# The two tiles of normed activations begin at 96 instead of 160 modulo 256 bytes

## The chip, the cores and the metric

The kernel runs on one core of a Trainium2 chip. The metric is the device time of one execution in microseconds (us). The engines are named as in the profile: PE is TensorE (matrix products), PEld its loading of weights, DVE VectorE, ACT ScalarE, POOL GpSimd, and SP the engine that issues most of the loads. On-chip memory has 128 partitions; a tile takes the same bytes of each, and an address below is a byte address inside a partition. "Residue" means that address modulo 256.

In a product, one operand is loaded into the array as weights (128 rows, up to 128 columns) and the other, the moving operand, streams past it (up to 512 columns).

## The reference

One decoder layer for 256 tokens of 1024 channels in float32: a half-weighted SwiGLU block, a mixer of two parallel branches, and a second SwiGLU block. Each has a norm in front and one behind.

```python
h = h + 0.5 * rmsnorm(swiglu(rmsnorm(h, ffn1_pre_g), w_gate, w_up, w_down), ffn1_post_g)
u = rmsnorm(h, mix_pre_g)
z, xbc, dt_raw, q, k, v, gate_logits = split(u @ w_in)       # 1024 x 10272
y_ssd = ssd_branch(z, xbc, dt_raw, ...)                       # state-space branch, 2048 wide
y_att = diff_attn_branch(q, k, v, ...)                        # differential attention, 8 heads
gates = sigmoid(gate_logits + gate_b)
h = h + rmsnorm((gates[0] * y_ssd + gates[1] * y_att) @ w_out, mix_post_g)
h = h + 0.5 * rmsnorm(swiglu(rmsnorm(h, ffn2_pre_g), ...), ffn2_post_g)
```

`swiglu(x) = (silu(x @ w_gate) * (x @ w_up)) @ w_down` with an inner width of 2816.

## The kernel before

Each product is computed in three parts for precision: both operands are split into a high part, rounded to the type fp32r, and the low rest, and high x high, high x low and low x high are added in PSUM. The weights come from DRAM in 122 chunks of 1 MB, each into one of 3 buffers of the group `raw` (8192 bytes per partition). ACT rounds a chunk to `whi` (line 167) and DVE subtracts to get `wlo` (line 168), two tiles each of 4096 bytes in the group `k4`, which has 29 buffers. Chunks are taken in one fixed order, with loads three chunks ahead and splits about three. PE's order is written out by hand in most stages.

The normed activations, transposed so that channels lie on partitions, stand in two tiles of the group `u8`, 8192 bytes each: `u0` has channels 0 to 511, `u1` the rest. Their shape is [128, 4, 2, 256]: four channel blocks, then the high and the low part, then 256 tokens. So the high and the low part of a block lie next to each other, and a matmul can stream 512 columns, both parts, or only the 256 of one. `new_u` allocates the pair anew for each of the three stages, `f1`, `mx` and `f2`. The second half of the attention's output also uses a buffer of this group, late in the mixer.

Four forms of product read u:

- `mm_w` (lines 215 to 218, tiles `pg_f` and `pup_f`): the FFN's gate and up products from the third chunk of 256 columns on. For each half m of the chunk's 256 columns, and for each of 8 channel blocks, the weights `whi` (128 columns) with 512 moving columns of u (line 216), and `wlo` with the 256 of the high part (line 215, or 218 for the first block).
- `mm_t` (lines 201, 202, 204, tiles `pbc`, `pxs`, `pz`, `pq`, `pk`): the mixer's products that are wanted transposed. Weights `whi` or `wlo`, 256 moving columns of u.
- `mm_nat` (line 231, tiles `pn_f`, `pn_mx`, `pgt`): u is loaded as weights, 128 tokens at a time, and 512 columns of `whi` or `wlo` stream. The same line also serves `pws` and `pwd`, which read the branches' outputs instead of u, and part of `pn_f`, which reads `raw_u`, a copy in `k4`.
- the time-step product `pdt` (lines 692 to 694): weights of 32 columns, `wdt_h` and `wdt_l`, 256 moving columns of u. Its weights of one channel block begin 128 bytes behind those of the block before.

The down product (`acc_f`, line 441) reads `gh_f` and `gl_f` of `k4` as weights and streams 512 columns of `whi` or `wlo`; it does not read u. Transposes on PE load the tile to be turned as weights and stream the identity matrix `ident`.

At the start, POOL builds `ident` and other constants, then computes the first norm's scale (lines 330 and 331) from sums that ACT and DVE make, and scales the second token block.

The built program places the tiles as follows (first byte of each buffer; residue modulo 256 in brackets):

```
                          before                 after
ident                     26240 (128)            the same
h                         18048 (128)            the same
raw, 3 buffers            35744 ... (160)        the same
gap0, 192 bytes           -                      60320 (160)
u8, 2 buffers             60320, 68512 (160)     60512, 68704 (96)
gap1, 64 bytes            -                      76896 (96)
k4, 29 buffers            76704 ... (160)        76960 ... (160)
squares, 2 buffers        195808 ... (224)       196064 ... (224)
k2, 7 buffers             200224 ... (32)        200480 ... (32)
k3, 3 buffers             214560 ... (32)        214816 ... (32)
```

So "all other tiles" of the change's title are the large ones that hold weights and activations, `raw` and `k4`; the constants and the small groups have residues of their own and keep them. All residues in the table are multiples of 32; those of u and the weights are 32 modulo 64 before and after.

Of the kernel before, what the change touches and what calls it, by code (L numbers as in the profile page):

```python
# [14 lines left out]
F32 = mybir.dt.float32  # L15
# [9 lines left out]
P = 128  # L25
# [23 lines left out]
def tile_hybrid_layer(ctx: ExitStack, tc: tile.TileContext, x, ffn1_pre_g, ffn1_w_gate, ffn1_w_up,  # L49
# [4 lines left out]
    nc = tc.nc  # L54
    const = ctx.enter_context(tc.tile_pool(name="const", bufs=1))
    sb = ctx.enter_context(tc.tile_pool(name="sb", bufs=1))
# [254 lines left out]

    uT = [None] * 2

    def new_u(tag):
        for i in range(2):
            uT[i] = sb.tile([P, 4, 2, T], F32R, tag="u8", name=f"u{i}_{tag}", bufs=2)

    act_u = (lambda j: uT[j // 4][:, j % 4, 0, :], lambda j: uT[j // 4][:, j % 4, 1, :],
             lambda j: uT[j // 4][:, j % 4, :, :])
# [146 lines left out]
    class Norm:  # L466
# [3 lines left out]
        def __init__(self, tag, g):  # L470
            self.tag, self.g, self.pus = tag, g, []
            new_u(tag)
            self.to0 = in_u(0)
            self.dr = None
            self.left = []
# [717 lines left out]
```

## Time and profile before

| | |
|---|---|
| median of 3 runs | 754.04 us (753.83 to 754.93) |
| profiled execution, first to last instruction | 753.1 us |
| PE busy | 743.7 us, 4377 matmuls |
| PEld busy | 646.1 us, 4377 loads |
| DVE, ACT, POOL busy | 521.7, 440.1, 38.2 us |
| granted clock of PE | 0.999 |
| bytes moved by DMA | 137.96 MB |

The median of the runs stands 0.94 us above the profiled execution's span, which has no time of its own beside that span; sums are made against the span and carried over with this difference.

How to read it: PE's matmuls are pipelined, so the recorded duration of one is longer than the distance from its start to the next one's start. What counts for the time is the distance. A group's row gives the number of instructions and the mean duration; a tile's rows give the minimum, median and maximum. A timeline row merges neighbours of the same kind; its first number is the start of the first.

### The profile page before, as it was taken

Reading aid. Unit: us, or ns where it says so; the run is one execution under the profiler, and the core shown is the slowest. Engines: PE = TensorE matmul, PEld = TensorE weight load, DVE = VectorE, ACT = ScalarE, POOL = GpSimd, SP = SyncE. Lnnn points to the kernel's source line nnn. Section 1 sums busy time; section 2 is a strip of 40 time slices with the busy share of each in tenths; the row PEclk is TensorE's granted clock in tenths of the full one; section 3 lists DMA queues with packets and bytes.
Section 4 is the critical chain, followed back from the end, with each engine's and each line's share of the span. In section 5 each row is a group of like instructions: output and inputs, shape, how many; then the busy total and the mean of one; then the engine's idle time right before and its main releaser. Section 6 shows DMA issues by size and latency. Waiting matters only on the chain.

```text
span 753.1 us, 11054 instructions
## 1 busy us (share of the span) xinstructions
PE 743.7 (99%) x4377; PEld 646.1 (86%) x4377; DVE 521.7 (69%) x792; ACT 440.1 (58%) x737; POOL 38.2 (5%) x72
## 2 busy tenths in 40 slices
PE   8999999999999999999999999999999999999996
PEld 6888888888889999898999788788888888888885
DVE  6686677654577978767778988695684867766612
ACT  7475566643565565858966556784463756565511
POOL 6400000000300000000000000000010000000000
PEclk9999999999999999999999999999999999999999
DMA  8685765587253556565555463467361776555701
GB/s 300 161 265 182 224 224 207 200 286 228 64 166 116 174 163 215 165 210 176 187 168 177 165 219 127 153 224 251 112 225 56 224 224 217 173 173 183 290 1 56
DMA packets 94212, 137.96 MB, mean 183 GB/s; under 512 B 2684, under 2 KB 68304, under 8 KB 94160
## 3 DMA queue, kind: packets, MB, share of 16 engines
q1 hardware_dynamic: 91488, 129.51, 52.5%
q0 software_dynamic: 2368, 7.22, 3.1%
q8 instruction: 34, 0.56, 0.3%
q10 hardware_dynamic: 304, 0.53, 0.2%
q14 instruction: 18, 0.15, 0.1%
HBM read 136.17 MB, written 1.08 MB: 182 GB/s over the span
## 4 chain that ended last, share of the span: by engine, by line
PE 96%; DVE 1%; DMA 1%; POOL 1%; ACT 1%; issue 0%; SPq 0%; DVEq 0%; POOLq 0%
PE acc_f L441 16%; PE pup_f L216 9%; PE pg_f L216 9%; PE pws L231 6%; PE pgt L231 6%; PE pn_f L231 5%; PE pg_f L215 4%; PE pup_f L215 4%; PE acc_mx L441 3%; PE pn_mx L231 3%; PE pwd L231 3%; PE pxs L204 2%; PE pxs L202 2%; PE pxs L201 2%; PE pz L204 2%; PE pz L201 2%
## 5 line engine op out<-in xcount | busy, mean ns | idle before, releaser
L168 DVE TENSOR_TENSOR wlo<-raw,whi 128x1024 fp32r<-128x1024 f32 (+1 forms) x246 | 291.6, 1214 | 56.3 <-ACT whi L167 53.6
L167 ACT CAST whi<-raw 128x1024 fp32r<-128x1024 f32 (+1 forms) x246 | 247.3, 1044 | 59.9 <-PE acc_f L441 21.8
L216 PE MATMUL pg_f<-u_f,whi 128*128 128x512 f32 x288 | 101.2, 396 | 0.0
L216 PE MATMUL pup_f<-u_f,whi 128*128 128x512 f32 x288 | 101.1, 396 | 0.0
L215 PE MATMUL pg_f<-u_f,wlo 128*128 128x256 f32 x252 | 70.5, 280 | 0.0
L215 PE MATMUL pup_f<-u_f,wlo 128*128 128x256 f32 x252 | 70.3, 279 | 0.0
L216 PEld LDWEIGHTS pg_f<-u_f,whi 128*128 128x128 f32 x288 | 52.9, 188 | 9.7
L216 PEld LDWEIGHTS pup_f<-u_f,whi 128*128 128x128 f32 x288 | 52.7, 188 | 9.8
L441 PE MATMUL acc_f<-whi,gh_f 128*128 128x512 f32 x176 | 58.2, 390 | 0.0
L441 PE MATMUL acc_f<-wlo,gh_f 128*128 128x512 f32 x176 | 58.1, 389 | 0.0
L441 PE MATMUL acc_f<-whi,gl_f 128*128 128x512 f32 x176 | 58.1, 389 | 0.0
L215 PEld LDWEIGHTS pg_f<-u_f,wlo 128*128 128x128 f32 x252 | 47.5, 188 | 1.7
L215 PEld LDWEIGHTS pup_f<-u_f,wlo 128*128 128x128 f32 x252 | 47.5, 189 | 1.6
L220 DVE TENSOR_TENSOR su_f<-pup_f,su_f 128x256 f32<-128x256 f32 x36 | 15.2, 423 | 38.7 <-ACT su_f L219 38.7
L441 PEld LDWEIGHTS acc_f<-whi,gl_f 128*128 128x128 f32 x176 | 33.0, 188 | 6.9
L441 PEld LDWEIGHTS acc_f<-wlo,gh_f 128*128 128x128 f32 x176 | 33.0, 188 | 6.8
L441 PEld LDWEIGHTS acc_f<-whi,gh_f 128*128 128x128 f32 x176 | 33.0, 188 | 6.8
L231 PE MATMUL pgt<-whi,u_mx 128*128 128x512 f32 x128 | 34.8, 400 | 0.0
L201 PE MATMUL pz<-u_mx,whi 128*128 128x256 f32 x128 | 32.3, 288 | 0.0
L202 PE MATMUL pz<-u_mx,whi 128*128 128x256 f32 x128 | 31.8, 284 | 0.0
L201 PE MATMUL pxs<-u_mx,whi 128*128 128x256 f32 x128 | 31.7, 285 | 0.0
L202 PE MATMUL pxs<-u_mx,whi 128*128 128x256 f32 x128 | 31.4, 283 | 0.0
(318 smaller groups left out, 1425.9 us busy)
## 6 DMA issues: line engine op xcount, KB each, us to landing
raw<-in_w_in_dram SPq DMA_DIRECT2D x40, 1024.0 KB, 5.4
raw<-in_ffn_w_down_dram SPq DMA_DIRECT2D x22, 1024.0 KB, 5.3
raw<-in_ffn_w_gate_dram SPq DMA_DIRECT2D x20, 1024.0 KB, 5.7
raw<-in_ffn_w_up_dram SPq DMA_DIRECT2D x20, 1024.0 KB, 6.1
raw<-in_ssd_w_branch_dram SPq DMA_DIRECT2D x8, 1024.0 KB, 5.0
acb<-acd POOLq DMA_DIRECT2D x8, 512.0 KB, 4.9
raw<-in_da_w_branch_dram SPq DMA_DIRECT2D x4, 1024.0 KB, 5.1
raw<-in_w_out_dram SPq DMA_DIRECT2D x4, 1024.0 KB, 4.9
```

The costliest lines, as they stand in the source:

```text
L167: nc.scalar.copy(hi[:, js, :], r[:, q * nj + j:q * nj + j + n, :])
L168: nc.vector.tensor_sub(lo[:, js, :], r[:, q * nj + j:q * nj + j + n, :], hi[:, js, :].bitcast(F32))
L201: nc.tensor.matmul(acc[m], wh(j)[:, cs], ah(k0 + j), start=first and j == ks[0], stop=False)
L202: nc.tensor.matmul(acc[m], wh(j)[:, cs], al(k0 + j), start=False, stop=False)
L204: nc.tensor.matmul(acc[m], wl(j)[:, cs], ah(k0 + j), start=False, stop=last and j == ks[-1])
L215: nc.tensor.matmul(acc[:, :T], wl(j)[:, cs], ah(j), start=False, stop=False)
L216: nc.tensor.matmul(acc, wh(j)[:, cs], ahl(j), start=j == 0, stop=j == KD - 1)
L220: nc.vector.tensor_tensor(dst[:, m, :], acc[:, :T], dst[:, m, :], ALU.add)
L231: nc.tensor.matmul(acc, a(k0 + j), b(j), start=first and i == 0, stop=last and i == 11)
L441: nc.tensor.matmul(acc[b][q], x_[:, ts], w_(kt)[:, halves[q]], start=i == 0 and kt == 0 and x_ is ah and w_ is wh, stop=i == n - 1 and kt ...
```

## The change

`new_u` allocates two more tiles that nothing reads: `gap0` of 192 bytes ahead of the pair, and `gap1` of 64 bytes behind it. Each is set to zero once by POOL. The pair then begins 192 bytes later, and all that comes behind it 256 bytes later.

```diff
     uT = [None] * 2

+    def gap(name, size):
+        nc.gpsimd.memset(sb.tile([P, size // 4], F32, tag=name, name=name, bufs=1), 0.0)
+
     def new_u(tag):
+        if uT[0] is None:
+            gap("gap0", 192)
         for i in range(2):
             uT[i] = sb.tile([P, 4, 2, T], F32R, tag="u8", name=f"u{i}_{tag}", bufs=2)
+            if tag == "f1" and i == 1:
+                gap("gap1", 64)
```

The order of instructions changes on POOL alone. There the program's start reads before, from the constant `nhalf` to the second scaling of the second token block (`un_f`):

```order
L285 MEMSET nhalf 128x1
L287 MEMSET ones 128x128
L280 ISA
L280 AFFINE_SELECT ident<-ident 128x128
L330 TENSOR_SCALAR r_f_119<-ss_f_114 128x1
L331 TENSOR_TENSOR r_f_119<-r_f_119,nhalf 128x1
L330 TENSOR_SCALAR r_f_127<-ss_f_122 128x1
L331 TENSOR_TENSOR r_f_127<-r_f_127,nhalf 128x1
```

The same place after the change, where the lines behind the new function have moved by 7 (330 is now 337):

```order
L285 MEMSET nhalf 128x1
L287 MEMSET ones 128x128
L280 ISA
L280 AFFINE_SELECT ident<-ident 128x128
L315 MEMSET gap_110 128x48
L315 MEMSET gap_114 128x16
L337 TENSOR_SCALAR r_f_123<-ss_f_118 128x1
L338 TENSOR_TENSOR r_f_123<-r_f_123,nhalf 128x1
```

The two memsets stand between the select that makes `ident` and the first norm's scale, with no wait of their own; PE, DVE, ACT and SP issue the same instructions in the same order as before.

## The prediction

> **What bounds the kernel now.** I read the page first, then the chain of waits, then single tiles and the timeline of TensorE, because the change touches nothing but addresses and the page alone cannot show what an address costs. The page and its chain:
>
> ```profile
> span 753.1 us, 11054 instructions
> PE 743.7 (99%) x4377; PEld 646.1 (86%) x4377; DVE 521.7 (69%) x792; ACT 440.1 (58%) x737; POOL 38.2 (5%) x72
> PEclk9999999999999999999999999999999999999999
> PE 96%; DVE 1%; DMA 1%; POOL 1%; ACT 1%; issue 0%; SPq 0%; DVEq 0%; POOLq 0%
> ```
>
> TensorE is busy 743.7 of 753.1 us at the full granted clock, and 96% of the chain is its own work. So only two things can move the time: the distance from one matmul to the next, or a new wait in front of one. The distances are read from single tiles (duration of one in ns, minimum, median, maximum) and from starts in the timeline and the chain:
>
> ```profile
> L692 PE MATMUL pdt<-u_mx,wdt_h x8: 276/276/281, 219.8 to 222.2; 128*32 128x256 f32 x8
> L204 PE MATMUL pxs<-u_mx,wlo x128: 283/283/283, 249.7 to 296.4; 128*128 128x256 f32 x128
> L441 PE MATMUL acc_f<-whi,gh_f x176: 389/389/477, 136.0 to 746.0; 128*128 128x512 f32 x176
> L231 PE MATMUL pgt<-wlo,u_mx x64: 389/389/395, 410.0 to 459.2; 128*128 128x512 f32 x64
> L231 PE MATMUL pws<-wlo,yh x64: 387/389/398, 463.5 to 514.4; 128*128 128x512 f32 x64
> L216 PE MATMUL pg_f<-u_f,whi x288: 389/395/403, 34.4 to 681.1; 128*128 128x512 f32 x144
> L215 PE MATMUL pg_f<-u_f,wlo x252: 274/280/384, 35.0 to 680.9; 128*128 128x256 f32 x126
> ...
> 249.91 0.96 PE pxs L204 x8
> ...
> 160.02 0.61 PE L441 MATMUL acc_f<-wlo,gh_f 128*128 128x512 f32 x2
> 160.47 0.62 PE L441 MATMUL acc_f<-whi,gh_f 128*128 128x512 f32 x2
> 160.93 0.62 PE L441 MATMUL acc_f<-whi,gl_f 128*128 128x512 f32 x2
> ...
> 220.15 0.28 PE L692 MATMUL pdt<-u_mx,wdt_h 128*32 128x256 f32 x1
> ...
> 220.60 0.28 PE L693 MATMUL pdt<-u_mx,wdt_h 128*32 128x256 f32 x1
> ```
>
> A duration holds a fixed part beside the distance to the next start: four `acc_f` matmuls take 160.93 - 160.02 = 0.91 us, 227 ns each, and last 389; four `pdt` take 0.45 us, 113 ns each, and last 276; eight `pxs` take 0.96 us, 120 ns each, and last 283. The fixed part is 162 to 163 ns each time, so a difference of durations is a difference of distances. The reader is to see a floor and a surplus. The floor is 113 ns for 256 moving columns and 227 for 512. `pdt` reaches it with u as moving tile and 32 columns of weights. `pxs`, the same u and the same 256 columns with 128 columns of weights, is 7 ns above it. With 512 moving columns `acc_f`, `pgt` and `pws` are at the floor, and the mixed stream of the FFN (`pg_f`, `pup_f`) lies between. So a load of 128 columns beside a moving read can cost some ns; whether the addresses of the two reads have a part in that is the whole question.
>
> **The change part by part.**
>
> *Two memsets on POOL.* They are issued behind the select that makes `ident` and ahead of the first line-330 operation:
>
> ```profile
> 0.79 0.20 POOL L279 MEMSET ident<- 128x128 f32 x1 [0.29 <-POOLq L1179]
> 0.94 0.10 POOL L283 MEMSET eps_c<- 128x1 f32 x1
> 1.25 0.28 POOL L280 TENSOR_SCALAR_AFFINE_SELECT ident<-ident 128x128 f32<-128x128 f32 x1
> 5.32 0.30 POOL L330 TENSOR_SCALAR r_f<-ss_f 128x1 f32<-128x1 f32 x1 [3.78 <-ACT sq_f L325]
> ```
>
> A memset of 1 column takes 0.10 us and one of 128 columns 0.20; 48 and 16 columns lie between, so both take 0.2 to 0.4 us, in an idle stretch of 3.78 us that ends when ACT has its sum. They neither wait for anything nor does anyone wait for their tiles. Cost 0; without that cover it would be 0.4 us at most, since POOL's products lead to TensorE's early transposes. No queue is passed by a moved step: nothing else is moved, on any engine.
>
> *256 bytes more of on-chip memory.* The last tile ends 256 bytes later and still fits; the number of buffers of every group is the same, so no buffer comes free earlier or later. Cost 0.
>
> *The weights' tiles and all behind them shift by 256 bytes.* Their residue modulo 256 is unchanged. Rows that speak for no effect of such a shift: the buffers of `whi` and `wlo` lie 4096 bytes apart in 29 places, a chunk uses now one, now another, and `pxs` line 204 is 283/283/283 over 128 matmuls. Cost 0.
>
> *u starts at residue 96 modulo 256 and the weights stay at 160.* This can act on every matmul that reads u. The counts, from three answers on the lines 201, 202 and 204 (TensorE's busy time and number of matmuls), then line 216, then line 231:
>
> ```profile
> 0.00:754.00 754.00, 111.89 (x448) 1.00 0.56 183
> 0.00:754.00 754.00, 110.49 (x448) 1.00 0.56 183
> 0.00:754.00 754.00, 64.31 (x448) 1.00 0.56 183
> 0.00:754.00 754.00, 196.79 (x576) 1.00 0.56 183
> 0.00:754.00 754.00, 184.85 (x768) 1.00 0.56 183
> ```
>
> The FFN's 576 wide matmuls stand in 72 blocks of 8 wide and 8 narrow ones, half of the blocks on the first 128 weight columns and half on the second. Starts of three blocks in a row (the row with x2 holds the last matmul of one block and the first of the next, 0.23 us later):
>
> ```profile
> 80.06 0.39 PE L216 MATMUL pg_f<-u_f,whi 128*128 128x512 f32 x1
> ...
> 82.64 0.63 PE L216 MATMUL pg_f<-u_f,whi 128*128 128x512 f32 x2
> ...
> 85.65 0.39 PE L216 MATMUL pup_f<-u_f,whi 128*128 128x512 f32 x1
> ```
>
> The first block takes 2.81 us, the second 2.78; at the floor it would be 8 x (227 + 113) = 2.72. So the bounds are these. If the new residue removed every surplus: 1344 x 7 ns = 9.4 us on lines 201 to 204, and 36 x 0.09 + 36 x 0.06 = 5.4 us in the FFN, 14.8 us in all. If it added a surplus of the same 7 ns to each matmul that can read u: 9.4 us on lines 201 to 204, at most 768 x 7 ns = 5.4 us on line 231 (some of these read other tiles), and as much again as now in the FFN, 5.4 us, 20 us in all. No row of this trace has u and 128 columns of weights at different residues in full-rate matmuls, so the value between is chosen by the nearest rows, and these are:
>
> ```profile
> L340 PE MATMUL pu_mx<-ident,h x8: 271/272/273, 191.8 to 192.5; 128*128 128x128 f32 x8
> L794 PE MATMUL px<-ident,xs x32: 272/273/328, 302.3 to 363.8; 128*128 128x128 f32 x32
> L917 PE MATMUL pa<-ident,s x24: 272/272/273, 433.9 to 506.5; 128*128 128x128 f32 x24
> ```
>
> In these transposes the moving tile `ident` is at residue 128, and the tile that is loaded as weights at 128 (`h`), 160 (`xs`) and 32 (`s`). All three have 272 to 273 ns. Likewise `pdt`: its weights advance by 128 bytes per matmul, so their residue alternates between 32 and 160 while u stays at 160, and minimum and median are both 276. Both kinds lack one thing, a surplus that could have gone. The third row is `pxs` itself: while DVE, ACT and the DMAs read and write at ever other addresses, its 128 matmuls show no spread at all. A collision by address would be expected to meet those accesses too and to leave some. I take 0 for this part.
>
> The Trainium skill's page "SBUF — State Buffer", section "Who interferes with whom", gives TensorE two read ports, one for the moving operand and one for the weights, and says that "PE and ACT never wait on anyone". This case's trace does not bear that out fully: `pxs` at 283 against `pdt` at 276 is a cost of loading weights beside a moving read. By the rule nothing would depend on addresses and the change would cost 0; a sum by the row alone leaves 0 to 14.8 us to be gained.
>
> Sum: 753.1 us of span, 0.94 us around it (the median of the runs is 754.04), change 0: 754.0.
>
> **The rivals.** *The collision goes by residue, and the new one avoids it (faster).* For it: the surplus exists, equal residues are the only case in which it is seen, and the FFN blocks differ by 0.03 us with the half of the weights that is used. Against it: the three rows above, and that `acc_f` and `pws` have equal residues too and no surplus. Its full price gives 754.0 - 14.8 = 739.2; half of the surplus 746.6; only the longer FFN blocks becoming like the shorter ones, 36 x 0.03 = 1.1 us, cannot be told from no change.
>
> *Equal residues are what keeps the 512-column matmuls at the floor (slower).* One mechanism: the load starts with the moving read, and streams that now run at a constant offset would meet at some other offset. For it: `pg_f` line 216 is at 395 where `acc_f` is at 389, so a wide matmul can be lengthened. Against it: `pgt` and `pws` are at 389 with u and with another tile as weights. Price: 7 ns on line 231's 768 gives at most 5.4 us, 759.4; with lines 201 to 204 as well, 768.8. It decides from 2 ns per line-231 matmul on, since 768 x 2 ns is 1.5 us.
>
> *The change does not do what it says.* Then the time is the same; the built program has the two tiles at 96 modulo 256, so this holds no chance of its own.
>
> **How the numbers follow.** A measurement here tells about 0.2%, 1.5 us, from no change. No effect within that: 0.55, the likeliest, hence 754.0. Collision avoided: 0.25, of which about 0.10 lies below 746 (nearly the full price). Collision added: 0.20, of which about 0.07 lies above 760. The range from 746 to 760 leaves out 0.17: it reaches down to half of the surplus removed and up to the full 7 ns on line 231. The likeliest case's own range is 752.5 to 755.5.
>
> **What would show it.** Right: the medians of `pxs`, `pgt`, `pg_f` and `pup_f` stay at 283, 389, 395 and 280, the blocks at 2.81 and 2.78, and line 330 still starts at about 5.3 us behind ACT. Wrong to the fast side: `pxs` at 276 to 280. Wrong to the slow side: `pgt` above 391, or `pxs` above 283. What would make the prediction wrong is a unit of 128 or 256 bytes in how TensorE's two reads share a path, which the transposes and `pdt` could not show because nothing collides there.

## The result and the profile after

The median fell from 753.93 to 749.03 us, of four runs each. The ratio is 0.9932, with a 95% interval of 0.9916 to 0.9948; it leaves out one run after the change, which took 1048.92 us at a granted clock of 0.655. The profiled execution has a span of 747.4 us and a time of 749.13 us. A distance of 1.7 to 1.8 us is found in each profiled execution from here on; the 0.94 us of the prediction set the span of one execution against the median of three, which moves nothing where the forecast is no change. The time lies inside the predicted range, but the likeliest case, no effect, did not come true. That it lies inside is owed to the range's lower end, which was drawn at half of the first rival's full price. The gain belongs to that rival, at about a third of its full price.

The page of the kernel after, head, busy times and the shares of the chain:

```profile
span 747.4 us, 11056 instructions
PE 737.6 (99%) x4377; PEld 639.1 (86%) x4377; DVE 521.4 (70%) x792; ACT 439.9 (59%) x737; POOL 38.9 (5%) x74
PE 96%; DVE 1%; DMA 1%; POOL 1%; ACT 1%; issue 0%; SPq 0%; DVEq 0%; ACTq 0%; POOLq 0%
```

The same 4377 matmuls keep TensorE busy for 6.1 us less, and 96% of the chain is still its own. So the time did not come out of a wait. It came out of the distances between matmuls. The tiles of the kernel after (duration of one in ns, minimum, median, maximum; first and last start; lines behind 316 are 7 higher than before):

```profile
L699 PE MATMUL pdt<-u_mx,wdt_h x8: 276/276/279, 220.0 to 222.4; 128*32 128x256 f32 x8
L201 PE MATMUL pbc<-u_mx,whi x64: 276/276/384, 222.7 to 245.9; 128*128 128x256 f32 x64
L204 PEld LDWEIGHTS pxs<-u_mx,wlo x128: 187/188/188, 248.7 to 293.0; 128*128 128x128 f32 x128
L204 PE MATMUL pxs<-u_mx,wlo x128: 276/276/276, 248.8 to 293.1; 128*128 128x256 f32 x128
L204 PE MATMUL pk<-u_mx,wlo x64: 276/276/282, 361.0 to 402.2; 128*128 128x256 f32 x64
L448 PE MATMUL acc_f<-whi,gh_f x176: 389/389/477, 136.0 to 740.4; 128*128 128x512 f32 x176
L231 PE MATMUL pgt<-wlo,u_mx x64: 388/392/394, 403.3 to 452.7; 128*128 128x512 f32 x64
L231 PE MATMUL pws<-wlo,yh x64: 387/389/397, 457.0 to 507.8; 128*128 128x512 f32 x64
L216 PE MATMUL pg_f<-u_f,whi x288: 388/397/398, 33.8 to 675.4; 128*128 128x512 f32 x144
```

Three rows of the kernel before that the prediction did not show stand against the second, the third and the fifth:

```profile
L201 PE MATMUL pbc<-u_mx,whi x64: 281/283/384, 222.5 to 246.6; 128*128 128x256 f32 x64
L204 PEld LDWEIGHTS pxs<-u_mx,wlo x128: 192/192/192, 249.6 to 296.3; 128*128 128x128 f32 x128
L204 PE MATMUL pk<-u_mx,wlo x64: 278/283/283, 365.9 to 408.9; 128*128 128x256 f32 x64
```

Read them in three groups. What streams 256 columns of u past 128 columns of weights fell by 7 ns, from a median of 283 to 276, where `pdt` was from the start; the load of the weights beside it (PEld) fell from 192 to 188. From the first `pbc` to the last `pk` it was 408.9 - 222.5 = 186.4 us, and is now 402.2 - 222.7 = 179.5: 6.9 us less. What loads u as weights and streams 512 columns became longer: `pgt` from 389 to 392. And the wide matmuls of the FFN became longer, `pg_f` from a median of 395 to 397. `acc_f` and `pws`, which do not touch u, kept their 389.

The chain of waits of the kernel after, in order of time, at the first `pxs`, and later where the transposes and the products of the state-space branch stand between the `pz`:

```profile
249.01 0.91 PE pxs L204 x8
...
338.36 0.22 PE py L828 x4
...
339.48 0.94 PE pz L204 x8
```

Eight `pxs` take 0.91 us, 113 to 114 ns each, where they took 0.96. But eight `pz` of the same form and the same residues take 0.94, 118 each. The floor is not reached everywhere.

Starts of the same three FFN blocks, from the timeline of TensorE after (in the row with x2 the second matmul begins the next block, 0.24 us later):

```profile
79.74 0.40 PE L216 MATMUL pg_f<-u_f,whi 128*128 128x512 f32 x1
...
82.31 0.63 PE L216 MATMUL pg_f<-u_f,whi 128*128 128x512 f32 x2
...
85.36 0.40 PE L216 MATMUL pup_f<-u_f,whi 128*128 128x512 f32 x1
```

Both blocks now take 2.81 us. The shorter kind, 2.78, is gone: of the 72 blocks 70 take 2.81 to 2.82 us, all but the first of each FFN stage. And the two memsets, from the timeline of POOL after:

```profile
1.51 0.17 POOL L315 MEMSET gap<- 128x48 f32 x2
5.35 0.31 POOL L337 TENSOR_SCALAR r_f<-ss_f 128x1 f32<-128x1 f32 x1 [3.68 <-ACT sq_f L332]
```

They take 0.17 us together, and the first norm's scale still waits for ACT behind them.

The parts of the change in span, from the distance of each matmul's start to the next one's, summed over each product in the two traces (us, after minus before):

| part | change |
|---|---|
| `pbc`, `pxs`, `pz`, `pq`, `pk` (lines 201 to 204) | -0.99 - 2.46 - 1.35 - 0.97 - 1.12 = -6.9 |
| `pg_f` and `pup_f` (lines 215 to 218) | +0.64 + 0.60 = +1.2 |
| `pn_f`, `pn_mx`, `pgt` (line 231, u as weights) | +0.20 + 0.15 + 0.25 = +0.6 |
| start of the program (`warm`, `pu_f`), before u exists | -0.7 |
| all else | +0.1 |
| span | 747.4 - 753.1 = -5.7 |

The start of the program is not the change's: the first `pg_f` starts at 34.4 us before, 33.8 after, and between 33.0 and 34.2 in the kernels below, whatever they change.

### The profile page after: what moved, and what is told of

It is laid out like the page before. It is cut to its first block, busy times and chain, and to the rows that moved or that the text cites. A ratio compares the mean times of both kernels' runs of the same rounds, so it can differ in the third digit from the quotient of the medians.

```text
span 747.4 us, 11056 instructions
## 1 busy us (share of the span) xinstructions
PE 737.6 (99%) x4377; PEld 639.1 (86%) x4377; DVE 521.4 (70%) x792; ACT 439.9 (59%) x737; POOL 38.9 (5%) x74
## 4 chain that ended last, share of the span: by engine, by line
PE 96%; DVE 1%; DMA 1%; POOL 1%; ACT 1%; issue 0%; SPq 0%; DVEq 0%; ACTq 0%; POOLq 0%
PE acc_f L448 16%; PE pup_f L216 9%; PE pg_f L216 9%; PE pgt L231 6%; PE pws L231 6%; PE pn_f L231 6%; PE pg_f L215 4%; PE pup_f L215 4%; PE pn_mx L231 3%; PE pwd L231 3%; PE acc_mx L448 3%; PE pxs L201 2%; PE pxs L202 2%; PE pxs L204 2%; PE pz L204 2%; PE pz L201 2%
## 5 line engine op out<-in xcount | busy, mean ns | idle before, releaser
L201 PE MATMUL pz<-u_mx,whi 128*128 128x256 f32 x128 | 31.2, 283 | 0.0
L202 PE MATMUL pz<-u_mx,whi 128*128 128x256 f32 x128 | 30.7, 279 | 0.0
L219 ACT COPY su_f<-pup_f 128x256 f32<-128x256 f32 x36 | 13.3, 369 | 29.5 <-PE pup_f L216 29.3
L201 PE MATMUL pxs<-u_mx,whi 128*128 128x256 f32 x128 | 30.2, 279 | 0.0
```

The costliest lines, as they stand in the source:

```text
L201: nc.tensor.matmul(acc[m], wh(j)[:, cs], ah(k0 + j), start=first and j == ks[0], stop=False)
L202: nc.tensor.matmul(acc[m], wh(j)[:, cs], al(k0 + j), start=False, stop=False)
L219: nc.scalar.copy(dst[:, m, :], acc[:, T:])
```

## The experiments

Theory A: a matmul's stream and the load of the next weights meet by the difference of their addresses modulo 256 bytes. Theory B: the residue of u alone counts. Theory C: something else in the edit moved, such as the memsets or the shift of all later tiles. A fourth question came with the answer: which difference is best for which form. Edits of the first three are against the kernel after, those of the mixer and the FFN against the kernel before.

**Shift alone.** Everything behind the gap moves by 256 bytes, u included.

```diff
-            gap("gap0", 192)
+            gap("gap0", 256)
-            if tag == "f1" and i == 1:
-                gap("gap1", 64)
```

> The changed kernel with both memsets and the shift by 256 bytes, but u back at residue 160: one unused tile of 256 bytes ahead of u and none behind it. If the residue of u is the cause: lines 201 to 204 at a median of 283 ns again, 754 us. If the memsets, or the move of the weights by 256 bytes, are the cause: 276 ns and 749 us.

This version has one memset, of 256 bytes, in place of the two. Measured: 754.19 us, ratio 1.0012 (0.9997 to 1.0028); two of its twelve runs took 759 us, and the profiled one 754.57. Its tile `pxs`:

```profile
L204 PE MATMUL pxs<-u_mx,wlo x128: 283/283/283, 249.5 to 296.1; 128*128 128x256 f32 x128
```

Each part of the table is within 0.1 us of before, the start of the program aside. The memset of the gap and the moved addresses cost nothing and bring nothing. Theory C falls.

**Both at 96.** u and the weights get the same new residue.

```diff
-            if tag == "f1" and i == 1:
-                gap("gap1", 64)
```

> Only the 192 bytes ahead of u: u at 96 and the weights at 96 too, so the two have equal residues again. If the difference between the residues of the moving tile and the weights counts: 283 ns on lines 201 to 204, 754 us. If the residue of u itself counts (96 instead of 160): 276 ns, 749 us or less.

Measured: 753.8 us, ratio 0.9998 (0.999 to 1.0007).

```profile
L204 PE MATMUL pxs<-u_mx,wlo x128: 283/283/283, 249.0 to 295.6; 128*128 128x256 f32 x128
```

u stands at 96 as in the kernel after, and nothing is gained. Theory B falls.

**Weights at 224.** u stays at 160, and the weights move instead, so that the difference is again -64.

```diff
-            gap("gap0", 192)
+            pass
```

> Only the 64 bytes behind u: u stays at 160, the weights go to 224, the same difference of -64 as in the changed kernel. If the difference counts: 276 ns on lines 201 to 204, the FFN's blocks at 2.81 us each, 749 us. If the residue of u itself counts: as the kernel before, 283 ns, 754 us.

Measured: 750.35 us, ratio 0.9949 (0.9937 to 0.9961).

```profile
L204 PE MATMUL pxs<-u_mx,wlo x128: 276/276/276, 248.0 to 292.3; 128*128 128x256 f32 x128
...
L231 PE MATMUL pgt<-wlo,u_mx x64: 388/392/394, 403.5 to 452.9; 128*128 128x512 f32 x64
```

The same marks as after, both the gain and the loss, with other residues and the same difference. Lines 201 to 204 gain 5.9 us instead of 6.9: `pz`, `pq` and `pk` stand more often at the distance between (225 of 358 `pz` distances below 150 ns are at 115 to 119 ns, 109 after). Why is open; here the residues of the small groups behind the weights move by 64 too, which in the kernel after they do not.

**A map by 16 bytes.** A kernel of its own in which no other engine works during the matmuls, at a granted clock of 1.0. The moving tile and the weights have the same residue, and the moving operand is read from 0 to 368 bytes further on; 40 matmuls for each offset, the offsets named `_a` (0) to `_x` (368). The forms are those of the kernel: t as `mm_t`, n as `mm_nat`, w as `mm_w`. In short:

```python
for off in OFFS:                      # in 4-byte elements: 0, 4, 8, ... 92
    lo, full = mv[:, 512*j + off:][:, :256], mv[:, 512*j + off:][:, :512]
    # t: matmul(a[:, :256], wt[:, j, :128], lo)
    # n: matmul(a, wt[:, j, :128], full)
    # w: matmul(a, either half of wt[:, j], full); matmul(a[:, :256], wt[:, j, :128], lo)
```

> None of the layer is computed: three kinds of streams by themselves, each for 24 offsets of the moving tile against the weights, in steps of 16 bytes from 0 to 368 (tiles _a to _x), 40 matmuls each (kind w: 40 pairs). Weights at residue 160. Kind t: 256 moving columns with 128 of weights; n: 512 with 128; w: 512 and 256 in turn. If the difference of residues counts by 64 bytes modulo 256: kind t has 283 ns at offset 0, 64 and 128 perhaps between, 276 at 192 (tile _m), and the same again 256 bytes on (_q as _a). If finer steps count, tiles inside 64 bytes differ. If it is a matter of the kernel's surroundings and not of these two reads: 276 everywhere, or 283 everywhere.

Some tiles of this kernel:

```profile
L87 PE MATMUL t_a<-mv,wt x40: 278/283/283, 18.9 to 23.6; 128*128 128x256 f32 x40
L87 PE MATMUL t_h<-mv,wt x40: 275/275/282, 52.2 to 56.6; 128*128 128x256 f32 x40
L87 PE MATMUL t_m<-mv,wt x40: 276/276/285, 75.7 to 80.1; 128*128 128x256 f32 x40
L87 PE MATMUL t_q<-mv,wt x40: 278/283/283, 94.4 to 99.1; 128*128 128x256 f32 x40
L92 PE MATMUL n_a<-mv,wt x40: 389/389/397, 132.2 to 141.1; 128*128 128x512 f32 x40
L92 PE MATMUL n_e<-mv,wt x40: 387/392/397, 169.2 to 178.2; 128*128 128x512 f32 x40
L89 PE MATMUL w_m<-mv,wt x40: 388/397/399, 523.0 to 536.8; 128*128 128x512 f32 x40
```

`t_a` is `pxs` before (283 at difference 0), and `t_m` is `pxs` after (276 at 192, that is -64). `t_q`, at 256, repeats `t_a`, and so do all offsets of t and n from 256 on repeat those from 0 to 0.1 ns: the period is 256 bytes. Where u is loaded as weights the sign turns, so `n_a` is `pgt` before (389 at 0) and `n_e` is `pgt` after (392 at 64). `w_m` is `pg_f` after, 397. The collision needs no DVE, ACT or DMA: it is between TensorE's own two reads. The mean distance to the next matmul (of the last half of each group, ns; for w the mean of a wide and a narrow one):

| offset in bytes | 0 | 16 | 64 | 112 | 128 | 192 | 208 | 224 | 240 | 256 |
|---|---|---|---|---|---|---|---|---|---|---|
| t | 120.0 | 118.7 | 117.8 | 113.3 | 118.7 | 113.3 | 119.5 | 118.3 | 117.0 | 120.0 |
| n | 226.7 | 231.7 | 228.9 | 231.2 | 232.6 | 233.3 | 234.7 | 233.3 | 226.7 | 226.7 |
| w | 176.8 | 173.3 | 176.6 | 176.7 | 175.5 | 176.7 | 175.0 | 173.3 | 176.7 | 173.3 |

The forms want different things. For t the floor of 113.3 is met at 112 and 192 alone, for n its floor of 226.7 at 0 and 240. Difference 0, the state before, is among the worst for t (120.0, as at 80 and 96) and among the best for n. The new difference, 192, is at the floor for t and with 176.7 among the longest for w. That is the table of parts above: a gain in the mixer, losses in the FFN and in line 231. Yet the offset does not fix everything: w takes 176.8 at 0 and 173.3 at 256, which is the same offset. A block of 8 wide and 8 narrow matmuls would last 16 x 176.8 = 2.83 us and 16 x 173.3 = 2.77, and the two kinds of FFN block before lasted 2.81 and 2.78.

**96 in the mixer alone.** From here on u has a padded buffer and a start of its own in each stage; the FFN's stays at 160.

```diff
-            uT[i] = sb.tile([P, 4, 2, T], F32R, tag="u8", name=f"u{i}_{tag}", bufs=2)
+            whole = sb.tile([P, 8 * T + 64], F32R, tag="u8", name=f"u{i}_{tag}", bufs=2)
+            o = {'f1': 0, 'mx': 192, 'f2': 0}[tag] // 4
+            uT[i] = whole[:, o:o + 8 * T].rearrange("p (c s t) -> p c s t", c=4, s=2)
```

> From the kernel before: u's two tiles get 256 bytes of room at their end, and in the mixer alone u begins 192 bytes in (residue 96); in both FFN stages it stays at 160. Sum from the changed kernel's parts: lines 201 to 204 -6.9 us, u as weights in the mixer +0.4, FFN 0: 6.5 us less than before, 747.5. If the FFN's streams were to depend on more than the difference, they would not come back to 2.82 and 2.78 us per block.

Measured: 747.24 us, ratio 0.9912 (0.9899 to 0.9926), span 745.7.

```profile
L216 PE MATMUL pg_f<-u_f,whi x288: 387/395/403, 33.4 to 673.7; 128*128 128x512 f32 x144
...
L204 PE MATMUL pxs<-u_mx,wlo x128: 276/276/277, 247.8 to 292.0; 128*128 128x256 f32 x128
```

The FFN is back at 395 and its parts within 0.1 us of before; lines 201 to 204 keep 6.8 us of gain. So the FFN's loss comes from u's new start in the FFN, and it is separable.

**176 in the FFN alone.** By the map, w at 16 bytes takes 173.3 ns.

```diff
+            o = {'f1': 16, 'mx': 0, 'f2': 16}[tag] // 4
```

> The other half: u begins 16 bytes in (residue 176) in both FFN stages and at 160 in the mixer. The streams by themselves had 173.3 ns per matmul for the FFN's mixture at a difference of 16, so blocks of 16 x 173.3 = 2.77 us instead of 2.82 and 2.78, and u as weights (difference -16 seen from the moving tile) at 227: 72 blocks x 0.024 = 1.7 us less than before, 752.3. If streams by themselves don't carry over to the kernel: no change, 754, or slower.

Measured: 752.7 us, ratio 0.9983 (0.9974 to 0.9992), span 751.0.

```profile
L216 PE MATMUL pg_f<-u_f,whi x288: 387/390/402, 33.6 to 679.0; 128*128 128x512 f32 x144
```

`pg_f` and `pup_f` gain 0.66 and 0.72 us, where 1.7 in all was expected; the products of `pn_f` that read u lose 0.16, and the mixer is as before. Nearly all blocks now take 2.775 to 2.779 us; 16 x 173.3 ns is 2.773.

**Both stages.** 176 in the FFN and 96 in the mixer.

```diff
+            o = {'f1': 16, 'mx': 192, 'f2': 16}[tag] // 4
```

> Both: residue 176 in the FFN stages, 96 in the mixer. If the stages add up: 6.5 + 1.7 = 8.2 us less than before, 745.8, ratio 0.989.

Measured: 746.01 us, ratio 0.9893 (0.988 to 0.9907), span 744.2. The parts add up: FFN -1.4, lines 201 to 204 -7.2, line 231 with u +0.6, `pn_f` with `raw_u`, which does not read u, -0.2, start of the program -0.6, together -8.8 of the -8.9.

```profile
L216 PE MATMUL pg_f<-u_f,whi x288: 387/390/398, 33.6 to 672.2; 128*128 128x512 f32 x144
```

**A map by 4 bytes.** As the first map, with 64 offsets from 0 to 252 bytes (`OFFS = list(range(64))`).

> As the first streams by themselves (no layer computed), but with 64 offsets in steps of 4 bytes, 0 to 252 (tiles _aa at 0 to _hh at 252, eight per first letter). If the two reads meet in pieces of 16 bytes, offsets within one piece give the same time, and kind t is at 276 ns for 112 to 124 and 192 to 204. If every element counts, they differ within a piece, and kind w may come below the 173.3 ns per matmul that was its least so far.

The first offsets of form t, 0, 4, 8 and 16:

```profile
L87 PE MATMUL t_aa<-mv,wt x40: 278/283/284, 19.0 to 23.7; 128*128 128x256 f32 x40
L87 PE MATMUL t_ab<-mv,wt x40: 278/287/289, 23.8 to 28.6; 128*128 128x256 f32 x40
L87 PE MATMUL t_ac<-mv,wt x40: 277/278/284, 28.7 to 33.2; 128*128 128x256 f32 x40
L87 PE MATMUL t_ae<-mv,wt x40: 275/276/277, 38.0 to 42.5; 128*128 128x256 f32 x40
```

Single elements count: 120.0 ns at 0, 123.3 at 4, 116.7 at 8. For t the floor of 113.3 is met at 16, 112, 144 and 192, and 123.3 is the most. For n only 0 has 226.7, and all others lie between 228.9 and 240.0. For w the least is 171.7, at 28, 60 and 236, the most 181.7. Of the 16 offsets that both maps have, most repeat to 0.5 ns, but nine of the 48 streams came out otherwise: t at 16, 128 and 144, n at 176 and 240, w at 0, 144, 208 and 224. Thus t at 16 has 113.3 (118.7 in the first map) and n at 240 has 236.7 (226.7). It is not chance from one stream to the next: behind the same neighbour, t at 16 took 118.7 three times (at 16 and at 272 in the first map, and in the kernel with other column counts below). Here another offset ran just ahead. So what a stream settles into seems to depend on what ran ahead of it too; no run changes that alone.

**Columns and type.** Weights of 32, 64 and 96 columns (x, y, z) and 128 in bf16 (h), 16 offsets in steps of 16 bytes.

```python
matmul(a[:c, :256], wt[:, j, :c], lo)        # x, y, z: c = 32, 64, 96
matmul(a[:, :256], wb[:, j, :128], lo_bf16)  # h
```

> Streams by themselves again (no layer computed), 16 offsets in steps of 16 bytes: 256 moving columns with 32 (x), 64 (y), 96 (z) and 128 (t) columns of weights in fp32r, and with 128 columns in bf16 (h). If the surplus comes from the load meeting the moving read, x is 276 ns at every offset, and the surplus appears and grows with the columns. If it comes from the start addresses alone, x shows it at the same offsets as t. In bf16, where each element is half as wide, a load that meets the moving read should show offsets too; if only the full rate of 4 bytes per column is short, h is the same at all.

```profile
L93 PE MATMUL x_a<-mv,wt x40: 280/280/281, 17.4 to 22.0; 128*32 128x256 f32 x40
L93 PE MATMUL x_b<-mv,wt x40: 275/275/276, 22.1 to 26.5; 128*32 128x256 f32 x40
L95 PE MATMUL h_a<-mb,wb x40: 272/273/282, 316.1 to 320.4; 128*128 128x256 bf16 x40
L95 PE MATMUL h_m<-mb,wb x40: 272/272/273, 368.6 to 372.8; 128*128 128x256 bf16 x40
```

For 32 columns neither branch of the expectation came: `x_a` at offset 0 has 280, 117.8 ns from start to start, and `x_b` at 16 has 275, where t has 118.7 ns. So narrow weights collide as well, only at fewer offsets: 9 of 16 are at the floor with 32 columns, 3 with 64, 2 with 96 and 2 with 128. In bf16 all 16 offsets take 109.2 ns.

**188 in the FFN, 96 in the mixer.** The least of w in the finer map, 171.7 ns at 28.

```diff
+            o = {'f1': 28, 'mx': 192, 'f2': 28}[tag] // 4
```

> As the version by stages, but u 28 bytes in (residue 188) in the FFN stages instead of 16. By the streams in steps of 4 bytes the FFN's mixture falls from 173.3 to 171.7 ns per matmul, 72 blocks x 16 x 1.6 = 1.9 us less on pg_f and pup_f, and u as weights (difference -28, 228) goes from 227 to 237.6, 144 x 11 = 1.6 us more on pn_f: 745.7, not to be told from 746.0, with the parts apart in the trace. If single elements don't carry over to the kernel, the parts stay.

Measured: 745.09 us, ratio 0.9881 (0.9864 to 0.9899), span 743.5: the shortest of all. Against 176 in the FFN, `pg_f` and `pup_f` gain 0.56 and 0.60 us more, where 1.9 was expected, since the blocks take 2.760 us and not 16 x 171.7 = 2.747. The products of `pn_f` that read u lose 0.18 more, where 1.6 was expected: the n stream's price at this offset does not carry over. The intervals of the two ratios overlap, so that this one is the better of the two rests on the parts in the traces.

```profile
L216 PE MATMUL pg_f<-u_f,whi x288: 387/389/398, 33.9 to 671.5; 128*128 128x512 f32 x144
```

## Why the prediction was right or wrong

**Right: what bounds the kernel.** The whole change of the span that is the edit's lies in distances between matmuls, and no wait came or went.

**Right: the terms of 0 for memsets, memory and the shift by 256.** The memsets take 0.17 us under the cover named, and the shift alone gave 1.0012 with 1 inside the interval.

**Wrong: "I take 0 for this part".** This step failed, and with it the chance of 0.55. It chose the value between its bounds by the nearest rows, and none of those rows could show the effect. `pdt` at residues 32 and 160 against 160 has differences of 128 and 0 with 32 columns. At its floor there, it said nothing of 128 columns: the map has 118.7 and 120.0 at these offsets with 128. Nor did it speak for 32 columns at 0, since a stream of its own at that offset has 117.8; why `pdt`, which takes the two offsets in turn, is at the floor is open. Whether fp32 transposes collide at any offset was not run. Rows in which a cost is absent were taken as rows against its depending on addresses. The text said so itself ("nothing collides there") and then went by them.

**Wrong: "A collision by address would be expected to meet those accesses too".** The first map has 283 at offset 0 while DVE, ACT and the DMAs are idle. The two reads that meet are TensorE's own. The zero spread of `pxs` is a stream that repeats one pattern with itself; it is a sign of a fixed difference, not of an absent collision. The Trainium skill's page "TensorE: Matmul & The Clock Gate", section "Step-by-step: what each phase is for", says that loading the next tile's weights "doesn't steal SBUF read bandwidth from the running matmul". For bf16 the runs agree (109.2 ns at 16 offsets in steps of 16 bytes); for the type of this kernel they do not (113.3 to 123.3 ns by the offset), and the measurement decides.

**First rival: mechanism right, size off.** Lines 201 to 204 were priced at 9.4 us and gave 6.9. They were not all at 283 before, and not all at 276 after: of `pz`'s 358 distances below 150 ns 243 are at 113 to 114 ns after, 109 at 115 to 119 and 6 above, as the row of 0.94 us shows. `pxs`, which runs long without another product between, came nearest to its price (384 x 7 ns = 2.7 us, measured 2.46). The FFN was priced at -5.4 us and gave +1.2. The price assumed that an offset good for one form is good for all, and the map shows that at 192 t is at its floor while w is at 176.7, near its longest. Of the price's 14.8 us the runs gave 4.9. The rival also read the two lengths of FFN block as going with the half of the weights. They do not: with a difference of 0 long and short blocks take turns, and the short ones are those of the second half in both FFN stages before, but those of the first half in the second FFN stage of three other kernels whose FFN has the same difference (the shift alone, both at 96, 96 in the mixer alone).

**Second rival: true as well, and small.** The equal residues did hold line 231's matmuls at the floor: `pgt` passed the 391 that was named, and the products with u as weights lost 0.6 us. The price of 7 ns was too high: the row shows 3 ns, and over all 192 matmuls of `pgt` the loss is 0.25 us, 1.3 ns each. The two rivals were weighed as exclusive, and both happened, in different products.

**What the prediction named as its way to fail is what happened.** A unit of 256 bytes in how the two reads share a path: the period is shown by `t_a` and `t_q`. What the smaller unit inside it is stays open: neighbours 4 bytes apart differ, and the same offset can settle at two distances. How the stretches of 118 ns in `pz` begin is not settled either: they stand behind other products in the chain, but with 96 in the mixer each time `pz` gained 1.35 us with the FFN's u at 96, 1.19 at 160, 1.63 at 176 and 1.62 at 188, each from one profile.

## What to carry to other kernels

Where a product in fp32r shows a distance some ns above that of another form with the same moving columns, the difference of the two operands' start addresses modulo 256 is worth a try, one start per stage and form, since what helps 256 columns can cost 512. A small stream of the exact form at each offset finds the candidates, and the kernel itself has to confirm them, since one offset can settle at two distances: the times expected with the maps' help for 176 in the FFN, for both stages and for 188 missed by 0.4, 0.2 and 0.6 us, and the parts of the last by more (1.2 us gained of 1.9, 0.2 lost of 1.6). And a row in which a cost is absent is no evidence on what the cost depends on: only two rows that have it, or one that has and one that should have it, are.

## What was unexpected of the hardware

- In fp32r two reads of one engine, the weights and the moving operand, lengthen a matmul by the difference of their addresses modulo 256 bytes: from 113.3 to 123.3 ns with 256 columns, 226.7 to 240.0 with 512. The load of the weights itself shows it: 192 ns before at `pxs` line 204, 188 after.
- Four bytes matter (120.0, 123.3 and 116.7 ns at 0, 4 and 8), though both operands are read in whole rows of 512 or 1024 bytes or more.
- An offset does not have one price: 176.8 and 173.3 ns for w at 0 and 256, 118.7 and 113.3 for t at 16 in two kernels. The FFN's two lengths of block, 2.81 and 2.78 us, at a difference of 0 look like the same thing.
- In bf16 nothing of this is seen, 109.2 ns at all 16 offsets in steps of 16 bytes, and the floor is 4 ns lower than in fp32r at the same number of columns.
